# Forming the feed-forward weights' sums in DRAM with adding transfers instead of on GpSimd

## The chip, the cores and the metric

The kernel runs on one core of one Trainium2 chip. The metric is the device time of one execution in microseconds (us), as the median of several runs. The engines are named as in the profile: PE is TensorE's matrix multiply and PEld its weight load, DVE is VectorE, ACT is ScalarE, POOL is GpSimd, SP is SyncE, which here only issues transfers. "Raw" means a piece of weights as it lies in DRAM, 128 partitions by 1024 fp32 numbers, 512 KB.

## What is computed

Two transformer blocks over 512 tokens of width 1024, all in fp32, one sequence. In order: dilated-window attention ("dil"), differential attention ("diff"), an mLSTM and RG-LRU mixer ("ev"), cross-attention to 256 memory rows ("x0"), a feed-forward ("ff0"), sliding-window attention with sinks ("sw"), a second cross-attention ("x1") and a second feed-forward ("ff1"). Each has a norm before it and one after it. What the change touches is the feed-forward, and the norm of the input:

```python
def squared_relu_mlp(u, w1, w2):
    return jnp.square(jax.nn.relu(u @ w1)) @ w2      # w1: 1024 x 4096, w2: 4096 x 1024

def rmsnorm(x, g):
    x32 = x.astype(jnp.float32)
    y = x32 * lax.rsqrt(jnp.mean(x32 * x32, axis=-1, keepdims=True) + EPS)
    return y.astype(x.dtype) * g
```

## The kernel before

**Products.** An fp32 product is made of three matmuls (`mm3`): each operand is split into a high and a low part, and high x high, high x low and low x high are summed. The weights of the whole program lie in DRAM as one stream of tiles, `ws`, in the order in which they are used (`stream_order`). A tile is two halves of 512 KB. `weights` hands out the next tile, and through it `_take`, `_fill` and `_load` (L286 to L301) run ahead: SP loads a half into one of three buffers `raw`, ACT makes its high part (`whi`, L443) and DVE its low part (`wlo`, L444), each in four buffers. All loads are issued by SP in program order, two halves ahead of the one being split (three in a feed-forward).

**The feed-forward's second product** (`ff`) is done by Strassen and Winograd's scheme with seven products in place of eight: the weights of w2 are cut into 16 blocks, eight for each of ff0 and ff1, each of four quarters B11, B12, B21, B22 of 512 KB. The scheme needs four sums of quarters, T1 to T4. In the main loop, one turn for each block, PE does two tiles of the first product (`unit`), ACT squares the result, POOL forms the sums of activations s1, S2, S3, S4 (L1491), and PE does the three products with B11, T1 and B21 of the block before. The other four (with T4, T2, T3 and B22, named S4, S2, S3 and A22 after their left operand) come after the loop, over all blocks, and use the banks one after the other.

**The sums of weights** are made by `block` and `block_end` with POOL: SP loads the four quarters into SBUF (`quad`), POOL subtracts them in pieces of 128x256 (`less`, L354), and T3, T2 and T4 are stored to DRAM (`T<-quad`) and loaded again later (`raw<-T`). B11, T1 and B21 are split straight from `quad`. The dilated stage uses `less` too, for other weights, and is not touched there.

**The end of the main loops.** When the last product with T3 (S3) of a token tile is done, `done` adds its bank to the tile `acc` with a DVE addition (L1522); the product with B22 then continues in the same bank, so PE waits for that addition. Boundaries (`boundary`) do the norm after the stage and prepare the next.

**The first norms.** `first_u` loads four tiles of 128 tokens; `norm_T` multiplies by the gain, a part of the columns on POOL (the `cut`) and the rest on DVE, takes the squares on ACT, forms the reciprocal root on POOL (L468, L469, tile `rs`) and scales on DVE (L483). PE then transposes.

**What sets the order.** Each engine works through its own list in the order in which a scheduler placed the instructions; a transfer issued by SP is hardware-queued, one by POOL software-queued. Each of these two kinds has eight completion lanes (DMAHW0 to 7, DMASW0 to 7), and a transfer waits for the one that used its lane eight transfers earlier.

Of the kernel before, what the change touches and what calls it, by code (L numbers as in the profile page):

```python
# [12 lines left out]
F32 = mybir.dt.float32  # L13
# [3 lines left out]
ALU = mybir.AluOpType  # L17
AX = mybir.AxisListType

P = 128  # L20
S = 512
D = 1024
# [191 lines left out]
class Prog:  # L214
    def __init__(self, ctx, tc, a, out, stages):
        self.tc, self.nc, self.a, self.out, self.stages = tc, tc.nc, a, out, stages
        nc = self.nc
# [5 lines left out]
        blocks, self.groups, rest = [], {}, []  # L223
        for n, (key, kind, sel) in enumerate(self.order):
            if kind != "quad":
                self.halves += rest + [(n, 0), (n, 1)]
                rest = []
            elif sel[2] == P:
                g = self.groups.setdefault(key, [])
                if sel[0] == 0:  # L230
                    g.append([n])
                elif sel[1] == 0:
                    g[-1].append(n)
                elif sel[0] == 768:
                    first = [(b, name) for name in ("B11", "B21") for b in g[-1]]
                    rest[-2:-2] = first[:2]
                    rest += first[2:]
                    rest += [(b, name) for name in ("T1", "T2", "B22", "T3", "T4") for b in g[-1]]
            elif sel[1] == 0:
                blocks.append(n)  # L240
                self.halves += [(b, name) for b in blocks[-2:-1] for name in ("B11", "T1", "B21")]
                if len(blocks) == 8:
                    late = [(b, name + "'") for name in ("B22", "T2", "T3", "T4") for b in blocks]
                    self.halves += late[:5] + [(n, name) for name in ("B11", "T1", "B21")] + late[5:]
                    blocks = []
# [11 lines left out]

        self.ident = self.cp.tile([P, P], F32, name="ident")
# [28 lines left out]
    def _load(self):  # L287

        while self.loaded < len(self.halves) and self.loaded < self.done + self.depth:
            n, name = h = self.halves[self.loaded]  # L290
            self.loaded += 1
            if isinstance(name, str) and name[-1] != "'":
                continue
            r = self.wt[h] = self.wp.tile([P, 1024], F32, tag="raw", name="raw", bufs=3)
            if name == "B22'":
                src = self.a["ws"][n + 1, :, 1024:]
            elif isinstance(name, str):
                src = self.wt[n][name]
            else:
                src = self.a["ws"][n, :, name * 1024:(name + 1) * 1024]  # L300
            self.nc.sync.dma_start(out=r, in_=src)  # L301
# [19 lines left out]
    def weights(self, key=None):  # L321
# [5 lines left out]
        n = self.pos  # L327
        assert key in (None, self.order[n][0]), (self.order[n][0], key)
        self.pos += 1
        got = self._take(2)  # L330
        c = 256 if self.order[n][1] == "cols" else 512
        return n, *(Halved([g[x].rearrange("p (k c) -> p k c", c=c) for g in got]) for x in range(2))

    def block(self, n, pool):

        q = self.wt[n] = {}

        def new(name):
            q[name] = pool.tile([P, 1024], F32, tag="quad", name="quad", bufs=5)

        for m, name in enumerate(("B11", "B12", "B21", "B22")):
            new(name)
            self.nc.sync.dma_start(out=q[name], in_=self.a["ws"][n + m // 2, :, (m % 2) * 1024:(m % 2 + 1) * 1024])
        new("T3")
        q["T1"], q["T2"], q["T4"] = q["B12"], q["B22"], q["B21"]
        self.less(q["T3"], q["B22"], q["B12"])
        self.less(q["T1"], q["B12"], q["B11"])
        self.less(q["T2"], q["B22"], q["T1"])
# [6 lines left out]

    def block_end(self, n):

        q = self.wt[n]
        self.less(q["T4"], q["B21"], q["T2"])
        for name in ("T3", "T2", "T4"):  # L360
            d = q[name + "'"] = self.dr.tile([P, 1024], F32, tag=name, name=name, bufs=8)
            self.nc.sync.dma_start(out=d, in_=q[name])
# [454 lines left out]
    def dil(self):  # L817
        nc = self.nc
        y = []
        self.v_phase("dil")  # L820
        with self.vg, self.pool("rt_dil") as rp, self.pool("dl") as p:
# [114 lines left out]
            self.cuts = 3, 6  # L936
            for hp in range(8):
# [520 lines left out]
    def ff(self, l, stage):  # L1458
# [9 lines left out]
        self.block(blocks[0], p)  # L1468
# [3 lines left out]
        banks = {}  # L1472

# [4 lines left out]
        def operands(w, n, x2):  # L1478
# [9 lines left out]
            for out, x, z, op in ((s1, ya[:, h[1]], left["A22"][:, n], ALU.add), (left["S2"][:, n], s1, ya[:, h[0]], ALU.subtract),  # L1488
                                  (left["S3"][:, n], ya[:, h[0]], ya[:, h[1]], ALU.subtract),
                                  (left["S4"][:, n], yb, left["S2"][:, n], ALU.subtract)):  # L1490
                nc.gpsimd.tensor_tensor(out=out, in0=x, in1=z, op=op)  # L1491
# [6 lines left out]
        def products(q, ops):  # L1498
# [9 lines left out]
            self.block_end(blocks[q])  # L1508
            if q < 7:
                self.block(blocks[q + 1], p)  # L1510
# [11 lines left out]
        add = lambda out, ps: nc.vector.tensor_tensor(out=out, in0=out, in1=ps, op=ALU.add)  # L1522

        def done(name, t):
            ps = banks[name if name == "S4" else "A11"][t]
            if name in ("S4", "S2"):
                add(part(t, 1), ps)
            if name == "S2":
                self.boundary(t, (part(t, 0), part(t, 1)), self.h[:, t, :], stage, bo[0])
            elif name == "S3":  # L1530
                add(part(2 + t, 1), ps)
# [17 lines left out]
        for k, (name, i) in enumerate(steps):  # L1549
            if k == 5:  # L1550
                products(7, ops)
                first.close()
                acc.update({t: p.tile([P, D], F32, tag="quad", name="acc", bufs=5) for t in (2, 3, 0, 1)})
# [156 lines left out]
    def first_u(self):  # L1710
# [4 lines left out]
        with self.pool("x0") as p:  # L1715
# [8 lines left out]
            steps = [self.norm_T(xt[t], self.gpre, self.u, t, p, 4, 384 if t else 0) for t in range(2)]  # L1724
# [76 lines left out]
```

## Time and profile before

| what | value |
|---|---|
| median of 3 runs | 2335.98 us (2335.03 to 2336.01) |
| profiled execution, its own time | 2335.89 us |
| its span, first to last instruction | 2334.1 us |
| PE busy | 2287.8 us, 98% |
| DVE, ACT, POOL busy | 1432.2, 1140.8, 744.9 us |
| moved by SP's queue | 305.19 MB, 39.0% of the transfer engines' time |
| granted TensorE clock, mean | 0.999 |

The share of busy time is of the span; between the execution's own time and its span lie 1.8 us. The granted clock is that of the profile's rows, 1.0 for 2.4 GHz and 0.5 for 1.2 GHz. The stages begin about here in the span: diff at 636 us, ev at 900, x0 at 1140, ff0 at 1310, sw at 1650, x1 at 1830, ff1 at 2020.

### The profile page before, as it was taken

To read this page: it belongs to the slowest core of one execution; us is meant where nothing else is said; L and a number is where in the kernel's file an instruction comes from. 1 tells how busy PE (TensorE), PEld (TensorE's weight loads), DVE (VectorE), ACT (ScalarE), POOL (GpSimd) and SP (SyncE) were. 2 spreads that over 40 slices of the span, in tenths; PEclk is the share of its full clock that TensorE was granted. 3 is DMA by queue.
4 is the path that set the end of the run, shared out by engine and by line. 5 is a ranking of instruction groups with operands and counts; after the bars stand their busy time and mean duration, and the time that the engine had idled before them with its cause. 6 is when DMAs were issued, how large, how long until landed. Compare 5 with 4: busy or idle time off the path is not lost.

```text
span 2334.1 us, 33247 instructions
## 1 busy us (share of the span) xinstructions
PE 2287.8 (98%) x12168; PEld 1871.5 (80%) x12168; DVE 1432.2 (61%) x2522; ACT 1140.8 (49%) x2337; POOL 744.9 (32%) x799
## 2 busy tenths in 40 slices
PE   7999999999999999999999999999999999999998
PEld 6887777777878878777898888887966988888887
DVE  7665666666565555774745554468777744644476
ACT  4443544555444444553434454456456533544464
POOL 5962212121221113000200466661211200577640
PEclk9999999999999999999999999999999999999999
DMA  6335343332432222222342355555332332455554
GB/s 234 131 116 167 106 132 104 111 97 83 143 103 90 90 89 94 76 73 99 122 149 72 119 190 198 190 185 203 126 93 97 136 109 73 154 198 187 192 199 172
DMA packets 101284, 309.26 MB, mean 132 GB/s; under 512 B 14348, under 2 KB 20524, under 8 KB 101120
## 3 DMA queue, kind: packets, MB, share of 16 engines
q1 hardware_dynamic: 100320, 305.19, 39.0%
q0 software_dynamic: 800, 1.94, 0.3%
q8 instruction: 96, 1.57, 0.3%
q14 instruction: 68, 0.56, 0.1%
HBM read 253.59 MB, written 33.55 MB: 123 GB/s over the span
## 4 chain that ended last, share of the span: by engine, by line
PE 61%; DVE 5%; POOL 2%; ACT 2%; issue 2%; DMA 1%; SPq 0%; POOLq 0%; DVEq 0%; ACTq 0%
PE pj L370 13%; PE pj L371 13%; PE pj L372 13%; PE sc L371 3%; PE sc L370 3%; PE sc L372 3%; DVE wlo L444 1%; PE pv L370 1%; PE pv L371 1%; PE pv L372 1%; PE sc L1657 1%; PE sc L1022 1%; DVE h L521 1%; PE pt L491 1%; POOL rs L469 1%
## 5 line engine op out<-in xcount | busy, mean ns | idle before, releaser
L444 DVE TENSOR_TENSOR wlo<-raw,whi 128x1024 fp32r<-128x1024 f32 x348 | 452.4, 1308 | 301.0 <-ACT whi L443 284.9
L370 PE MATMUL pj<-uh,whi 128*128 128x512 f32 (+1 forms) x1424 | 561.7, 394 | 0.2 <-ACT ho L1348 0.2
L372 PE MATMUL pj<-uh,wlo 128*128 128x512 f32 (+1 forms) x1424 | 552.2, 388 | 2.1 <-DVE wlo L444 2.1
L371 PE MATMUL pj<-ul,whi 128*128 128x512 f32 (+1 forms) x1424 | 551.6, 387 | 0.0
L443 ACT ACTIVATE whi<-raw 128x1024 fp32r<-128x1024 f32 x348 | 364.9, 1057 | 352.9 <-PE pj L371 150.3
L354 POOL TENSOR_TENSOR quad<-quad 128x256 f32<-128x256 f32 x352 | 345.7, 1019 | 84.8 <-DVE wlo L444 37.8
L370 PEld LDWEIGHTS pj<-uh,whi 128*128 128x128 f32 x1424 | 267.6, 188 | 72.2 <-issue 17.3
L372 PEld LDWEIGHTS pj<-uh,wlo 128*128 128x128 f32 x1424 | 267.6, 188 | 61.1 <-issue 3.8
L371 PEld LDWEIGHTS pj<-ul,whi 128*128 128x128 f32 x1424 | 267.8, 188 | 52.9 <-issue 3.4
L603 POOL TENSOR_TENSOR ro<-rt 128x512 f32<-128x512 f32 x74 | 127.4, 1737 | 512.4 <-DVE rt L601 415.2
L466 POOL TENSOR_SCALAR rs<-ss 128x1 f32<-128x1 f32 x32 | 23.9, 747 | 542.0 <-ACT bq L512 541.6
L444 DVE TENSOR_TENSOR wlo<-quad,whi 128x1024 fp32r<-128x1024 f32 x90 | 125.3, 1395 | 76.2 <-ACT whi L443 76.1
L370 PE MATMUL sc<-whi,yh 128*128 128x512 f32 x384 | 151.7, 395 | 2.7 <-DVE acc L1522 2.6
L371 PE MATMUL sc<-wlo,yh 128*128 128x512 f32 x384 | 151.4, 394 | 1.1 <-DVE wlo L444 1.0
L372 PE MATMUL sc<-whi,yl 128*128 128x512 f32 x384 | 150.6, 393 | 0.0
L370 PE MATMUL pj<-whi,yh 128*128 128x512 f32 x360 | 141.9, 394 | 0.0
L371 PE MATMUL pj<-wlo,yh 128*128 128x512 f32 x360 | 140.7, 391 | 0.7 <-DVE wlo L444 0.7
L372 PE MATMUL pj<-whi,yl 128*128 128x512 f32 x360 | 140.7, 391 | 0.0
L443 ACT ACTIVATE whi<-quad 128x1024 fp32r<-128x1024 f32 x90 | 95.0, 1058 | 85.8 <-PE pj L371 33.0
L370 PEld LDWEIGHTS sc<-whi,yh 128*128 128x128 f32 x384 | 72.3, 188 | 20.9 <-ACT whi L443 2.0
L371 PEld LDWEIGHTS sc<-wlo,yh 128*128 128x128 f32 x384 | 72.4, 189 | 17.1 <-DVE wlo L444 2.8
L372 PEld LDWEIGHTS sc<-whi,yl 128*128 128x128 f32 x384 | 72.5, 189 | 15.0 <-DVE yl L444 0.2
(420 smaller groups left out, 4434.3 us busy)
## 6 DMA issues: line engine op xcount, KB each, us to landing
raw<-in_ws_dram SPq DMA_DIRECT2D x300, 512.0 KB, 3.7
quad<-in_ws_dram SPq DMA_DIRECT2D x88, 512.0 KB, 6.2
T<-quad SPq DMA_DIRECT2D x48, 512.0 KB, 3.0
raw<-T SPq DMA_DIRECT2D x48, 512.0 KB, 3.8
qk<-ro SPq DMA_DIRECT2D x256, 64.0 KB, 2.0
vd<-vo SPq DMA_DIRECT2D x24, 256.0 KB, 3.9
gpre<-in_gains_dram SPq DMA_DIRECT2D x8, 512.0 KB, 5.2
v<-vd SPq DMA_DIRECT2D x8, 512.0 KB, 5.0
```

The lines of the kernel that those rows point to most:

```text
L354: self.nc.gpsimd.tensor_tensor(out=out[:, cs], in0=x[:, cs], in1=y[:, cs], op=ALU.subtract)
L370: self.nc.tensor.matmul(ps, lhsT=ah, rhs=bh, start=first and k == 0, stop=False, **kw)
L371: self.nc.tensor.matmul(ps, lhsT=ah, rhs=bl, start=False, stop=False, **kw)
L372: self.nc.tensor.matmul(ps, lhsT=al, rhs=bh, start=False, stop=last and k == n - 1, **kw)
L443: self.nc.scalar.activation(out=dst[0], in_=src, func=AF.Copy)
L444: self.nc.vector.tensor_sub(out=dst[1], in0=src, in1=dst[0].bitcast(F32))
L466: nc.gpsimd.tensor_scalar(out=r[:, 0:1], in0=ss[:, 0:1], scalar1=ss[:, 1:2], scalar2=EPS, op0=ALU.add, op1=ALU.add)
L469: nc.gpsimd.tensor_tensor(out=r[:, 1:2], in0=r[:, 0:1], in1=self.mhalf[:, 0:1], op=ALU.pow)
L491: nc.tensor.transpose(pt[:, k * P:(k + 1) * P], b[:, (4 * g + k) * P:(4 * g + k + 1) * P], self.ident)
L521: nc.vector.scalar_tensor_tensor(out=h, in0=b, scalar=r, in1=h, op0=ALU.mult, op1=ALU.add)
L603: nc.gpsimd.tensor_tensor(out=o, in0=t[0], in1=t[1], op=op)
L1022: nc.tensor.matmul(ps[:, :n], lhsT=q[hs, 0, i * P:n], rhs=q[hs, 1, :n], start=True, stop=True)
```

## The change

It removes `block` and `block_end`. A list of 128 steps (`sums`, 64 for each feed-forward) forms the same sums in DRAM: a step is either a plain copy of 512 KB, DRAM to DRAM, issued by SP, or a transfer that adds its source to a tile in DRAM (`accum_op=add`), issued by POOL. [...] `weights` issues one step for each tile it hands out, from the dilated heads on (`self.paced`), and what is left at the start of a feed-forward is issued there (`background`). By the list, the 64 steps of ff0 are issued by the end of ev's output weights; those of ff1 go with x0, ff0's first weights, sw and x1, and 3 are left at the start of ff1. Every piece, B11, T1 and B21 too, is now loaded as `raw`. At the end of S3, ACT copies the bank to a tile `u3` and POOL subtracts it in two pieces, in place of the DVE addition. The tiles `acc` have a tag of their own. In `first_u`, the first two norms use no POOL columns (the second had 384).

```diff
--- before.py
+++ after.py
@@ -220,7 +220,7 @@
         self.wt = {}
 
         self.halves, self.ready, self.loaded, self.done, self.depth = [], [], 0, 0, 2
-        blocks, self.groups, rest = [], {}, []
+        blocks, self.groups, rest, sums = [], {}, [], []
         for n, (key, kind, sel) in enumerate(self.order):
             if kind != "quad":
                 self.halves += rest + [(n, 0), (n, 1)]
@@ -238,10 +238,11 @@
                     rest += [(b, name) for name in ("T1", "T2", "B22", "T3", "T4") for b in g[-1]]
             elif sel[1] == 0:
                 blocks.append(n)
-                self.halves += [(b, name) for b in blocks[-2:-1] for name in ("B11", "T1", "B21")]
+                self.halves += [(b, name + "'") for b in blocks[-2:-1] for name in ("B11", "T1", "B21")]
                 if len(blocks) == 8:
                     late = [(b, name + "'") for name in ("B22", "T2", "T3", "T4") for b in blocks]
-                    self.halves += late[:5] + [(n, name) for name in ("B11", "T1", "B21")] + late[5:]
+                    self.halves += late[:5] + [(n, name + "'") for name in ("B11", "T1", "B21")] + late[5:]
+                    sums += self.sums(blocks)
                     blocks = []
 
         def pool(name, **kw):
@@ -255,6 +256,7 @@
         self.sm = pool("sm")
         self.dr = pool("dr", space=bass.MemoryType.DRAM)
 
+        self.todo, self.paced, self.summed = iter(sums), False, 0
         self.ident = self.cp.tile([P, P], F32, name="ident")
         make_identity(nc, self.ident)
         self.mhalf = self.cp.tile([P, 8], F32, name="mhalf")
@@ -292,8 +294,8 @@
             if isinstance(name, str) and name[-1] != "'":
                 continue
             r = self.wt[h] = self.wp.tile([P, 1024], F32, tag="raw", name="raw", bufs=3)
-            if name == "B22'":
-                src = self.a["ws"][n + 1, :, 1024:]
+            if isinstance(name, str) and name[0] == "B":
+                src = self.part_of(n, name)
             elif isinstance(name, str):
                 src = self.wt[n][name]
             else:
@@ -328,38 +330,46 @@
         assert key in (None, self.order[n][0]), (self.order[n][0], key)
         self.pos += 1
         got = self._take(2)
+        if self.paced:
+            self.background()
         c = 256 if self.order[n][1] == "cols" else 512
         return n, *(Halved([g[x].rearrange("p (k c) -> p k c", c=c) for g in got]) for x in range(2))
 
-    def block(self, n, pool):
-
-        q = self.wt[n] = {}
-
-        def new(name):
-            q[name] = pool.tile([P, 1024], F32, tag="quad", name="quad", bufs=5)
-
-        for m, name in enumerate(("B11", "B12", "B21", "B22")):
-            new(name)
-            self.nc.sync.dma_start(out=q[name], in_=self.a["ws"][n + m // 2, :, (m % 2) * 1024:(m % 2 + 1) * 1024])
-        new("T3")
-        q["T1"], q["T2"], q["T4"] = q["B12"], q["B22"], q["B21"]
-        self.less(q["T3"], q["B22"], q["B12"])
-        self.less(q["T1"], q["B12"], q["B11"])
-        self.less(q["T2"], q["B22"], q["T1"])
+    def part_of(self, n, name):
+
+        m, c = int(name[1]) - 1, int(name[2]) - 1
+        return self.a["ws"][n + m, :, c * 1024:(c + 1) * 1024]
+
+    def sums(self, blocks):
+
+
+        steps = ((("T1", "B11"), ("T3", "B22")), (("T1", "B12"), ("T3", "B12")), (("T2", "T1"),), (("T2", "B22"),),
+                 (("T4", "T2"),), (("T4", "B21"),))
+        return [(blocks[at - k], name, src, k % 2) for at in range(len(blocks) + 5) for k in (0, 2, 4, 1, 3, 5)
+                if 0 <= at - k < len(blocks) for name, src in steps[k]]
+
+    def background(self, n=1):
+
+        for _ in range(n):
+            step = next(self.todo, None)
+            if step is None:
+                return
+            b, name, src, adds = step
+            self.summed += 1
+            q = self.wt.setdefault(b, {})
+            src = self.part_of(b, src) if src[0] == "B" else q[src + "'"]
+            if adds:
+                ins = self.nc.gpsimd.dma_start(out=q[name + "'"], in_=src, accum_op=ALU.add)
+            else:
+                d = q[name + "'"] = self.dr.tile([P, 1024], F32, tag=name, name=name, bufs=16)
+                ins = self.nc.sync.dma_start(out=d, in_=src)
+            self.tc.keep_in_program_order(ins)
 
     def less(self, out, x, y):
         out, x, y = (z.rearrange("p a b -> p (a b)") if len(z.shape) == 3 else z for z in (out, x, y))
         for c in range(4):
             cs = slice(c * 256, (c + 1) * 256)
             self.nc.gpsimd.tensor_tensor(out=out[:, cs], in0=x[:, cs], in1=y[:, cs], op=ALU.subtract)
-
-    def block_end(self, n):
-
-        q = self.wt[n]
-        self.less(q["T4"], q["B21"], q["T2"])
-        for name in ("T3", "T2", "T4"):
-            d = q[name + "'"] = self.dr.tile([P, 1024], F32, tag=name, name=name, bufs=8)
-            self.nc.sync.dma_start(out=d, in_=q[name])
 
     def mm3(self, ps, pairs, first=True, last=True, between=None, **kw):
 
@@ -934,6 +944,7 @@
 
             osb = {}
             self.cuts = 3, 6
+            self.paced = True
             for hp in range(8):
                 if hp:
                     plan(hp - 1)
@@ -1465,11 +1476,11 @@
         p = outer.enter_context(self.pool(f"ff{l}"))
         self.depth = 3
         left = {n: p.tile([P, 16, 256], F32, name=n) for n in ("S3", "A22")}
-        self.block(blocks[0], p)
         p2 = inner.enter_context(self.pool(f"fs{l}"))
         left.update({n: p2.tile([P, 16, 256], F32, name=n) for n in ("S4", "S2")})
         p1 = first.enter_context(self.pool(f"fr{l}"))
         banks = {}
+        self.background(8 * 8 * (l + 1) - self.summed)
 
         def square(out, ps, tmp):
             nc.scalar.activation(out=tmp, in_=ps, func=AF.Relu)
@@ -1485,9 +1496,9 @@
             square(yb, ps[:, h[0]], yb)
             square(left["A22"][:, n], ps[:, h[1]], left["A22"][:, n])
             s1 = p1.tile([P, 256], F32, tag="s1", name="s1", bufs=3)
-            for out, x, z, op in ((s1, ya[:, h[1]], left["A22"][:, n], ALU.add), (left["S2"][:, n], s1, ya[:, h[0]], ALU.subtract),
+            for out, x, z, op in ((s1, ya[:, h[1]], left["A22"][:, n], ALU.subtract), (left["S2"][:, n], s1, ya[:, h[0]], ALU.subtract),
                                   (left["S3"][:, n], ya[:, h[0]], ya[:, h[1]], ALU.subtract),
-                                  (left["S4"][:, n], yb, left["S2"][:, n], ALU.subtract)):
+                                  (left["S4"][:, n], yb, left["S2"][:, n], ALU.add)):
                 nc.gpsimd.tensor_tensor(out=out, in0=x, in1=z, op=op)
             x1 = self.pair()
             res = {"A11": [z[:, h[0]] for z in x1], "A12": [z[:, h[1]] for z in x1], "S1": [z[:, h[n % 2]] for z in x2]}
@@ -1505,9 +1516,6 @@
                     tok = slice(t * P, (t + 1) * P)
                     self.mm3(banks[name][t], [([z[:, tok] for z in ops[j][name]], (hi[:, j, :], lo[:, j, :])) for j in range(2)],
                              first=q == 0, skip_group_check=True)
-            self.block_end(blocks[q])
-            if q < 7:
-                self.block(blocks[q + 1], p)
 
         ops = []
         for q in range(8):
@@ -1519,16 +1527,20 @@
         banks["S4"] = [self.ps("pj") for _ in range(2)]
         acc, bo, late = {}, [], []
         part = lambda t, c: acc[t][:, c * 512:(c + 1) * 512]
-        add = lambda out, ps: nc.vector.tensor_tensor(out=out, in0=out, in1=ps, op=ALU.add)
+        add = lambda out, ps, op=ALU.add: nc.vector.tensor_tensor(out=out, in0=out, in1=ps, op=op)
 
         def done(name, t):
             ps = banks[name if name == "S4" else "A11"][t]
             if name in ("S4", "S2"):
-                add(part(t, 1), ps)
+                add(part(t, 1), ps, ALU.add if name == "S4" else ALU.subtract)
             if name == "S2":
                 self.boundary(t, (part(t, 0), part(t, 1)), self.h[:, t, :], stage, bo[0])
             elif name == "S3":
-                add(part(2 + t, 1), ps)
+                o = bo[0].tile([P, 512], F32, tag="u3", name="u3", bufs=2)
+                self.copy(o, ps, "s")
+                for c in range(2):
+                    cs = slice(c * 256, (c + 1) * 256)
+                    nc.gpsimd.tensor_tensor(out=part(2 + t, 1)[:, cs], in0=part(2 + t, 1)[:, cs], in1=o[:, cs], op=ALU.subtract)
             elif name == "A22":
                 self.boundary(2 + t, (ps, part(2 + t, 1)), self.h[:, 2 + t, :], stage, bo[0])
 
@@ -1550,7 +1562,7 @@
             if k == 5:
                 products(7, ops)
                 first.close()
-                acc.update({t: p.tile([P, D], F32, tag="quad", name="acc", bufs=5) for t in (2, 3, 0, 1)})
+                acc.update({t: p.tile([P, D], F32, tag="acc", name="acc", bufs=4) for t in (2, 3, 0, 1)})
                 for t in range(2):
                     self.copy(part(2 + t, 1), banks["S1"][t], "s")
                 for t in range(2):
@@ -1721,7 +1733,7 @@
                     self.gpre = self.gain(p, GAINS[self.stages[0]][0], "gpre")
                 elif t == 1:
                     self._load()
-            steps = [self.norm_T(xt[t], self.gpre, self.u, t, p, 4, 384 if t else 0) for t in range(2)]
+            steps = [self.norm_T(xt[t], self.gpre, self.u, t, p, 4, 0) for t in range(2)]
             steps[0]()
             steps[1]("pj")
             steps = [self.norm_T(xt[t], self.gpre, self.u, t, p, 4, 384) for t in range(2, NT)]
```

At the start, POOL lists these before the change (`rs` are the reciprocal roots, `bu<-xt,gpre` the multiplication by the gain):

```order
L468 TENSOR_SCALAR rs<-ss_106 128x1 [waits Activation_49]
L480 TENSOR_TENSOR bu<-xt,gpre 128x384 [waits DMAHW2_49,DMAHW1_49]
L469 TENSOR_TENSOR rs<-rs,mhalf 128x1 [waits Pool_49]
L468 TENSOR_SCALAR rs<-ss_115 128x1 [waits Activation_49]
L469 TENSOR_TENSOR rs<-rs,mhalf 128x1 [waits Pool_49]
L480 TENSOR_TENSOR bu<-xt,gpre 128x384 [waits DMAHW5_49]
```

And these with it:

```order
L478 TENSOR_SCALAR rs<-ss_106 128x1 [waits Activation_49]
L479 TENSOR_TENSOR rs<-rs,mhalf 128x1 [waits Pool_49]
L478 TENSOR_SCALAR rs<-ss_115 128x1 [waits Activation_49]
L479 TENSOR_TENSOR rs<-rs,mhalf 128x1 [waits Pool_49]
L490 TENSOR_TENSOR bu<-xt,gpre 128x384 [waits DMAHW5_49,DMAHW1_49]
```

The multiplication between the two steps of the first root is gone from POOL; DVE does all 1024 columns of the second tile.

Where the differential stage begins, POOL listed these before the change (`mask_d`, `tmp<-in_lam_dram` and `subln` are small transfers which that stage needs):

```order
L468 TENSOR_SCALAR rs<-ss_5860 128x1 [waits Activation_49]
L469 TENSOR_TENSOR rs<-rs,mhalf 128x1 [waits Pool_49]
L627 DMA mask_d<-in_mask_d_dram 128x512 [waits DMASW1_49,DMASW0_49,DVE_49]
L992 DMA tmp<-in_lam_dram 128x256
L627 DMA subln<-in_subln_dram 128x1
```

And these with it:

```order
L478 TENSOR_SCALAR rs<-ss_5906 128x1 [waits Activation_49]
L479 TENSOR_TENSOR rs<-rs,mhalf 128x1 [waits Pool_49]
L362 DMA T_4242<-in_ws_dram 128x1024 [waits DMASW5_49]
L362 DMA T_4377<-in_ws_dram 128x1024 [waits DMASW6_49]
L637 DMA mask_d<-in_mask_d_dram 128x512 [waits DMASW7_49,DVE_49]
L1003 DMA tmp<-in_lam_dram 128x256 [waits DMASW0_49]
L637 DMA subln<-in_subln_dram 128x1 [waits DMASW1_49]
L613 TENSOR_TENSOR ro<-rt 128x512 [waits DVE_49] x2
L362 DMA T_4560<-in_ws_dram 128x1024 [waits DMASW2_49]
```

Two adding transfers stand ahead of the small ones, and each of the small ones waits for a lane.

In x0, where the memory's weights are used, SP's list with the change is this (before it holds the rows `raw` alone):

```order
L365 DMA T_10405<-in_ws_dram 128x1024 [waits DMAHW2_49]
L303 DMA raw<-in_ws_dram 128x1024 [waits DMAHW7_49,DVE_49]
L303 DMA raw<-in_ws_dram 128x1024 [waits DMAHW0_49,DVE_49]
L365 DMA T_10632<-in_ws_dram 128x1024 [waits DMAHW5_49]
L303 DMA raw<-in_ws_dram 128x1024 [waits DMAHW1_49,DMAHW6_49,DVE_49,Activation_49]
L303 DMA raw<-in_ws_dram 128x1024 [waits DMAHW3_49,DVE_49]
L365 DMA T_10711<-in_ws_dram 128x1024
L303 DMA raw<-in_ws_dram 128x1024 [waits DMAHW4_49,DVE_49,Activation_49]
L303 DMA raw<-in_ws_dram 128x1024 [waits DMAHW6_49,DMAHW2_49,DVE_49]
L365 DMA T_10790<-in_ws_dram 128x1024
```

A copy now stands ahead of every two loads, and the loads wait for the lanes that copies use too.

## Rows read from the trace of the kernel before

**Rows 1.** The page: busy us of each engine, and SP's queue (packets, MB, share).

```profile
PE 2287.8 (98%) x12168; PEld 1871.5 (80%) x12168; DVE 1432.2 (61%) x2522; ACT 1140.8 (49%) x2337; POOL 744.9 (32%) x799
...
q1 hardware_dynamic: 100320, 305.19, 39.0%
```

**Rows 2.** POOL's row L354 alone, in ff0 and ff1: busy us (instructions).

```profile
1300.00:1600.00 300.00, 118.14 (x128) 1.00 0.54 189
2000.00:2300.00 300.00, 119.20 (x128) 1.00 0.57 196
```

**Rows 3.** Stretches of 50 us; busy us (count): PE, PEld, DVE, ACT, POOL; clock; DMA.

```profile
1450.00:1500.00 50.00, 50.00 (x222) 41.40 (x221) 24.35 (x22) 23.88 (x43) 36.47 (x43) 1.00 0.55 189
1550.00:1600.00 50.00, 49.34 (x216) 39.95 (x215) 42.70 (x45) 33.52 (x46) 16.95 (x15) 1.00 0.61 215
1600.00:1650.00 50.00, 47.40 (x219) 38.33 (x218) 39.28 (x44) 30.00 (x46) 12.74 (x13) 1.00 0.46 164
2250.00:2300.00 50.00, 49.24 (x214) 39.49 (x213) 41.52 (x51) 34.87 (x51) 4.47 (x7) 1.00 0.70 241
```

**Rows 4.** PE's waits over the whole run: total us, times, longest.

```profile
PE pt L491 <- DVE bu L483: 17.7, 7, 11.8
```

**Rows 5.** Timeline of the start: start us, us, instruction [idle before it, what ended it].

```profile
5.82 1.23 DVE L480 TENSOR_TENSOR bu<-xt,gpre 128x1024 f32<-128x1024 f32 x1 [5.82 <-DMA gpre<-in_gains_dram]
8.70 0.83 DVE L480 TENSOR_TENSOR bu<-xt,gpre 128x640 f32<-128x640 f32 x1 [1.65 <-DMA xt<-in_x_dram]
...
8.81 1.56 POOL L480 TENSOR_TENSOR bu<-xt,gpre 128x384 f32<-128x384 f32 x1 [2.83 <-DMA xt<-in_x_dram]
...
10.94 0.75 DVE L483 TENSOR_SCALAR bu<-bu,rs 128x1024 f32<-128x1024 f32 x1 [1.42 <-POOL rs L469]
...
11.75 1.54 PE L491 MATMUL pt<-ident,bu 128*128 128x128 f32 x6 [11.75 <-DVE bu L483]
```

**Rows 6.** Timeline, last block of ff0: POOL's sum, then PE.

```profile
1538.12 4.00 POOL L354 TENSOR_TENSOR quad<-quad 128x256 f32<-128x256 f32 x4 [2.96 <-DVE wlo L444]
...
1573.65 0.50 PE L371 MATMUL pj<-wlo,yh 128*128 128x512 f32 x1 [0.37 <-DVE wlo L444]
```

**Rows 7.** Timeline, end of S3 in ff0, and a POOL piece of 128x256.

```profile
1623.58 0.68 DVE L1522 TENSOR_TENSOR acc<-acc,sc 128x512 f32<-128x512 f32 x1
...
1624.41 0.47 PE L370 MATMUL sc<-whi,yh 128*128 128x512 f32 x1 [1.60 <-DVE acc L1522]
...
1542.08 0.74 POOL L1491 TENSOR_TENSOR s<-ya,A 128x256 f32<-128x256 f32 x1
```

**Rows 8.** The page, transfers: out<-in, issuing queue, count, KB, median us to landing.

```profile
raw<-in_ws_dram SPq DMA_DIRECT2D x300, 512.0 KB, 3.7
...
T<-quad SPq DMA_DIRECT2D x48, 512.0 KB, 3.0
...
qk<-ro SPq DMA_DIRECT2D x256, 64.0 KB, 2.0
```

**Rows 9.** Timeline, start of diff: POOL's issues, and DVE waiting for one.

```profile
635.12 0.95 POOL L627 DMA_DIRECT2D mask_d<-in_mask_d_dram  x1
636.08 0.55 POOL L992 DMA_DIRECT2D tmp<-in_lam_dram  x1
...
639.50 0.36 DVE L996 TENSOR_TENSOR tmp<-tmp 128x64 f32<-128x64 f32 x2 [0.82 <-DMA tmp<-in_lam_dram]
...
641.62 0.69 DVE L601 TENSOR_TENSOR rt<-sc,cos 128x512 f32<-128x512 f32 x1 [0.82 <-PE sc L372]
```

**Rows 10.** Memory weights of x0: a stretch, and ACT waiting for a load.

```profile
1160.00:1194.70 34.70, 34.70 (x292) 34.70 (x290) 20.20 (x22) 16.10 (x20) 0.00 (x0) 1.00 0.58 196
...
1164.95 1.06 ACT L443 ACTIVATE whi<-raw 128x1024 fp32r<-128x1024 f32 x1 [2.93 <-DMA raw<-in_ws_dram]
```

**Rows 11.** Timeline, start of sw: SP's issues of q and PE's first score.

```profile
1695.53 5.46 SPq L1640 DMA_DIRECT2D q<-ro  x8
...
1702.39 0.48 PE L1657 MATMUL sc<-kd,q 64*128 64x128 f32 x2
```

## Prediction

> **What bounds the kernel now.** I read the page first: PE is busy 2287.8 of 2334.1 us [rows 1], so some 46 us are all that can come from any wait, and the change leaves PE's matmuls as they are. POOL is the engine that the change relieves: the pieces of row L354 in the two feed-forwards take 118.14 and 119.20 us [rows 2], all removed. The next view, stretches of 50 us, tells whether they bound anything. In the main loop of ff0 PE is busy 50.00 of 50.00 us with 222 matmuls, while POOL has 36 us [rows 3]: POOL is not the bound there, and removing it gives nothing. Only the edges are not full. From 1550 PE does 216 matmuls in place of 222, which is 6 x 0.225 = 1.35 us; from 1600 it is idle 2.60 us; in ff1 from 2250 it does 214, so 1.8 us [rows 3]. So the feed-forwards can give 5.75 us at most. Last I read PE's waits: the longest is the start, 11.8 us for the first scaled tile [rows 4].
>
> The profiled execution took 2335.89 us, 0.09 under the median of the runs; its span is 1.8 us less. I make the sum against it.
>
> **First norms.** POOL's multiplication begins at 8.81 and ends at 10.37; the root's second step stands behind it, so DVE scales at 10.94 after idling 1.42, and PE starts at 11.75 [rows 5]. The change takes the multiplication out from between. The root is then done before DVE is free; DVE multiplies 1024 columns where it did 640, 1.23 us for 0.83 [rows 5], from 8.70 to 9.93, and scales right behind. That is 10.94 - 9.93 = 1.0 us earlier. **-1.0** (0 if the weights then come late, to -1.4, the whole idle time).
>
> **Sums in the main loops.** 256 POOL pieces, 237.3 us [rows 2], lie beside a full PE: 0. SP's transfers change from 128 loads and 48 stores to 112 loads in the loops' time; the 64 copies and 64 additions lie earlier. PE stays full: 0. The edge of the last block is another matter: there the sum of 4.00 us runs at 1538, and the low parts of later weights come late, costing PE 0.37 us at 1573.65 [rows 6] and some smaller gaps, 1.35 us in the stretch [rows 3]. Without quarters to load and store the loads come sooner. I take **-1.0** of the 1.35 for ff0; in ff1 part of the 1.8 us is a wait for a bank, which stays, and I take **-0.5**.
>
> **End of S3.** PE waits 1.60 us for DVE's addition, which begins at 1623.58 behind a low part [rows 7]. A copy by ACT frees the bank earlier, so this goes. But ACT's next row then reads `acc`, which is ready only after two POOL pieces of 0.74 us [rows 7], and the high part of the next weights stands behind it on ACT: 1.5 us come back. **0** (from -1.6 to +1.5).
>
> **The new transfers.** The trace has no copy from DRAM to DRAM and no adding transfer, so I bound both. SP's queue moved 305.19 MB in 39.0% of the engines' time [rows 1]: 0.39 x 2334.1 / 305.19 x 0.524 = 1.56 us of all engines for 512 KB in one pass. A copy costs 1.56 if read and write go in one pass, 3.1 if in two. An addition reads twice and writes once: 1.56 to 4.7. I take the middles, 2.3 and 3.1; a store and a load, the nearest rows, land in 3.0 and 3.7 us with their fixed part [rows 8], which fits neither end better. On POOL an issue costs up to 0.95 [rows 9]; 64 of them are 61 us where 237 were removed.
>
> Where do 128 of these meet something? In the attention heads and the output products there is one step for each tile of at least 48 matmuls of 0.225 us, 10.8 us; with two loads (3.1) and a step (4.7 at worst) it is under 8 us: 0. The exception is the memory's weights, eight tiles in each of x0 and x1. Their matmuls are half as long: 34.70 us for 292 [rows 10], 0.119 each, 48 for a tile, 5.7 us. Loads already land just in time there (ACT idles 2.93 for one at 1164.95) [rows 10]. With two loads at 1.56 and a step: by my middles x0 has 6 copies and 2 additions, 20 + 25 = 45 us of 45.6, and x1 3 and 5, 22.4 + 25 = 47.4. There are about 3 us of slack in the split pieces. So it just fits, and I take **+0.5** for x0 and **+0.7** for x1 as the odd late load.
>
> The Trainium skill ("DMA: Bandwidth & Descriptors", Latency and other measured facts) gives 207 to 214 GB/s for copies between tensors in DRAM whose row pitch is not one of the slow ones; by it, an estimate, a copy is 2.5 us, which no run here shows yet. By that the sum of x0 would be 1 us longer and no more.
>
> **Small transfers at two edges.** Two additions now stand ahead of `mask_d`, `lam` and `subln` on POOL. Behind two issues of 0.95 the lam arrives 2 us later than 639.50, and DVE, which waits for it, has until 641.62 when PE's next result comes [rows 9]: nearly free. But the 64 KB transfers after it land in 2.0 us alone [rows 8], and the diff stage's first score and the first score of sw (PE at 1702.39, the issue of the last q ending 1701) [rows 11] follow the landing without slack. A copy in their way delays them by part of its 2.3 us: **+0.5** each, +1.0 (0 to +4).
>
> **Sum:** -1.0 - 1.0 - 0.5 + 0 + 0.5 + 0.7 + 1.0 = -0.3, so 2335.89 - 0.3 = **2335.6 us**. A measurement of this kernel tells some 0.2% from no change, 4.7 us.
>
> **Rivals.**
>
> *B, slower: transfers fill the engines with the memory's weights.* Place: eight tiles of x0 and of x1. It decides from 5.7 - 2 x 1.56 = 2.6 us for a step on. At the high bounds, 3.1 and 4.7, x0 needs 25 + 6 x 3.1 + 2 x 4.7 = 53 us of 45.6, x1 25 + 3 x 3.1 + 5 x 4.7 = 57.8: +7.4 and +12.2, less 3 us of slack each, about +13.6. With the gains of the forecast that gives **2349 us**. For it: loads land just in time there, at 0.58 share of the transfer engines [rows 10]. Against: a store into DRAM is no slower than a load [rows 8], so one direction is cheap. The Trainium skill ("Collectives: The Full Stack", The bandwidth ceiling: the fold count and why AG ≠ RS ≠ AR) says that an adding transfer needs two source reads through one ring and runs at about half of a copy's rate; by it and the page's figure for copies an addition would be some 4.9 us, an estimate, which is this rival's end. No row of before has such a transfer. **17%.**
>
> *C, faster: all edges fill up and nothing comes late.* -1.0 at the start, -1.35 in ff0's last block, -1.6 at S3 (ACT has time for the pieces), -0.8 in ff1: -4.75, **2331.1 us**. For it: each of these waits has a row [rows 3, 5, 7]. Against: ACT's order behind S3. **13%.**
>
> *D, a little slower: small transfers queue behind big ones.* Every 64 KB transfer on a path without slack (first scores of diff and sw, lam) waits for a whole copy or addition, 1.6 to 3.1 us each, two or three times: +3 to +7 with nothing gained at S3, **2341 us**. For it: completion lanes are shared, so a small transfer waits for the one eight earlier. Against: most small transfers land long before their use. **12%.**
>
> *A, the forecast*, to which belongs that the change does not do what it says, because POOL's work was hidden all along [rows 3]: **58%.**
>
> **How the numbers follow.** The likeliest is A, 2335.6. The range reaches down to C (2331.0) and up through D, into the half of B's span where only x1 overflows (+12.2 - 3 = +9.2): 2345.0. Above it lies most of B, some 12%, and below it some 6%. Faster by over 0.2% means under 2331.3: half of C and a sliver of A, 0.10. Slower means over 2340.7: B, half of D and the rest from A's upper end, 0.24. Same: 0.66.
>
> **What would show it.** Right: DVE's first scaling at about 9.9 and PE's first row at 10.7; POOL without rows of L354 after the dilated weights; the stretch 1450 to 1500 with 222 matmuls as before; in the page's list of transfers a copy that lands in 3 to 5 us. B shows as waits of PE or ACT for `raw` in x0 and x1 and a transfer share near 1 there; D as a later first score in diff and sw; C as stretches 1550 to 1650 with 222 matmuls each. Wrong would be any loss in the main loops, which I count as full, or a term of over 3 us in the dilated heads.

## The result, and the profile after

The changed kernel takes **2372.57 us** (median of 4 runs, 2365.73 to 2373.6) against 2335.67 (4 runs of before): slower, 1.0146 times, interval 1.0134 to 1.0158. I had forecast 2335.6 and a range to 2345. The profiled execution took 2365.73, the shortest of the four; what follows accounts for its 30 us, not for the 37 of the median.

The page of the changed kernel: busy time, the queues, and the transfers with their time to landing.

```profile
PE 2301.4 (97%) x12168; PEld 1880.5 (80%) x12168; DVE 1411.2 (60%) x2518; ACT 1143.4 (48%) x2341; POOL 564.6 (24%) x614
...
q1 hardware_dynamic: 96736, 305.19, 38.4%
q0 software_dynamic: 10016, 35.49, 8.9%
...
T<-in_ws_dram POOLq DMA_DIRECT2D x64, 512.0 KB, 7.4
...
T<-in_ws_dram SPq DMA_DIRECT2D x32, 512.0 KB, 5.6
```

POOL lost 180 us of work, and SP's queue moves the same bytes [rows 1]. The adding transfers are the growth of queue q0. PE is busy 13.6 us longer with the same 12168 matmuls [rows 1], and the mean granted clock is 0.991 in place of 0.999; the other 16 us of the 30 are idle time. PE's waits over the whole run, those that are new against [rows 4]:

```profile
PE sc L1033 <- DMA qk<-ro: 6.1, 1, 6.1
PE pj L381 <- DVE wlo L454: 4.0, 5, 0.9
...
PE sc L1669 <- DMA q<-ro: 2.4, 1, 2.4
PE pj L380 <- ACT whi L453: 2.2, 3, 1.0
```

PE's order is the same in both kernels but for two matmuls that come eight places earlier, so each matmul's start can be subtracted from that of before. The difference changes in few places ("half clock" is a granted clock of 0.5, 1.2 GHz):

| place (time in before) | change of the delay, us | what is seen there |
|---|---|---|
| start to 577 | -2.8 | scaling earlier; no half-clock stretch at 574 |
| first score of diff, 654 | +10.3 | wait of 6.1, then half clock |
| ev, 940 and 975 | +3.1 | small tables (`rgw` and others) late behind an addition, +1.5; half clock, +1.6 |
| memory's norm ahead of x0, 1109 | +2.4 | wait of 2.6 in place of 1.8; half clock |
| memory's weights of x0, 1171 to 1175 | +4.7 | three waits, half clock |
| ff0 | -1.2 | -1.2 last block, -1.9 and +1.9 at S3 |
| first scores of sw, 1703 | +5.9 | wait of 2.4, then half clock |
| memory's weights of x1, 1855 to 1869 | +7.6 | waits, half clock |
| ff1 and between the places | -0.2 | |

Together +29.8, and the spans differ by 29.9. The main loops are as full as before, 222 matmuls in 50 us. Stretches of the changed kernel (columns as in [rows 3], then GB/s):

```profile
650.00:660.00 10.00, 3.91 (x13) 2.36 (x11) 2.35 (x3) 0.50 (x2) 1.80 (x2) 0.84 0.87 227
660.00:670.00 10.00, 10.00 (x31) 6.46 (x32) 4.35 (x17) 3.00 (x8) 0.00 (x0) 0.65 0.08 32
...
1860.00:1900.00 40.00, 35.21 (x262) 33.93 (x261) 20.45 (x23) 16.39 (x22) 9.86 (x11) 0.91 0.97 253
1450.00:1500.00 50.00, 50.00 (x222) 41.42 (x221) 21.50 (x23) 26.02 (x48) 12.20 (x16) 1.00 0.49 148
```

The kernel before, at the place of the first two rows:

```profile
650.00:660.00 10.00, 10.00 (x45) 7.19 (x45) 5.41 (x17) 3.63 (x10) 0.00 (x0) 1.00 0.66 203
```

The second row of the changed kernel is the one that I had no term for: the wait is over, PE is busy all 10 us, the transfers are quiet (0.08), and yet the granted clock is 0.65, so a part of the stretch ran at 1.2 GHz and only 31 matmuls were done. Of the 10.3 us at this place 6.1 are the wait and 4.2 come behind it. Over the run the 13.6 us of longer busy time are this part: matmul by matmul, 14.9 us are lost in half-clock stretches, and before lost 1.5 in its one at 574.

What made the first score late, on the timelines of POOL, DVE and PE:

```profile
632.34 1.84 POOL L362 DMA_DIRECT2D T<-in_ws_dram  x2
633.84 0.94 POOL L637 DMA_DIRECT2D mask_d<-in_mask_d_dram  x1
634.45 0.90 POOL L1003 DMA_DIRECT2D tmp<-in_lam_dram  x1
...
646.44 4.53 POOL L613 TENSOR_TENSOR ro<-rt 128x512 f32<-128x512 f32 x2 [10.55 <-DVE rt L611]
650.91 0.90 POOL L362 DMA_DIRECT2D T<-in_ws_dram  x1
```

```profile
642.63 0.36 DVE L1007 TENSOR_TENSOR tmp<-tmp 128x64 f32<-128x64 f32 x2 [6.72 <-DMA tmp<-in_lam_dram]
```

```profile
657.63 0.76 PE L1033 MATMUL sc<-qk 64*128 64x128 f32 x2 [6.09 <-DMA qk<-ro]
```

`lam`, issued at 634.45, lands 8.1 us later, just behind the second addition (641.68); before it took 3.4 [rows 9]. DVE idles 6.72 for it with the rotations queued behind. A third addition, issued at 650.91, then runs beside the eight 64 KB pieces of `qk`: the first four land 1.9 to 2.1 us after their issue, the last four 4.1 to 5.5.

At sw one addition stood beside the pieces of `q`, again on POOL's timeline:

```profile
1714.61 0.91 POOL L362 DMA_DIRECT2D T<-in_ws_dram  x1
```

The pieces issued up to then landed 2.0 us after their issue, the seven issued from 1715.26 to 1720.71 after 4.7 to 7.1 us.

And the additions of x1, on POOL's timeline:

```profile
1863.61 6.86 POOL L362 DMA_DIRECT2D T<-in_ws_dram  x8
```

All eight go out in 6.9 us, right behind the boundary's norm. By the list of steps they are the additions of x1's memory weights and of its queries, tiles that are used one after the other, long after the burst: SP's copies wait in line with the loads, but nothing ties an addition to its tile, and POOL issues all of them as soon as its list reaches them. From 1870.1 to 1897.5 they land one by one, some 3.9 us apart, and the raw loads beside them at 3.8 to 3.9, where tiles ask for two loads in 5.7 us.

### The profile page after: what moved, and what is told of

Same layout as the page of the kernel before. It is cut to its first block, busy times and chain, and to the rows that moved or that the text cites. A ratio compares the mean times of both kernels' runs of the same rounds, so it can differ in the third digit from the quotient of the medians.

```text
span 2364.0 us, 33064 instructions
## 1 busy us (share of the span) xinstructions
PE 2301.4 (97%) x12168; PEld 1880.5 (80%) x12168; DVE 1411.2 (60%) x2518; ACT 1143.4 (48%) x2341; POOL 564.6 (24%) x614
## 5 line engine op out<-in xcount | busy, mean ns | idle before, releaser
L454 DVE TENSOR_TENSOR wlo<-raw,whi 128x1024 fp32r<-128x1024 f32 x396 | 501.8, 1272 | 356.7 <-ACT whi L453 344.9
L453 ACT ACTIVATE whi<-raw 128x1024 fp32r<-128x1024 f32 x396 | 416.5, 1056 | 395.2 <-PE pj L381 189.0
L372 POOL TENSOR_TENSOR quad<-quad 128x256 f32<-128x256 f32 x96 | 108.3, 1168 | 0.0
L362 POOL DMA_DIRECT2D T<-in_ws_dram x64 | 55.2, 1027 | 149.2 <-DMA T<-T 109.2
L454 DVE TENSOR_TENSOR yl<-ya,yh 128x256 fp32r<-128x256 f32 x32 | 19.6, 613 | 118.5 <-ACT yh L453 118.5
```

The costliest lines, as they stand in the source:

```text
L362: ins = self.nc.gpsimd.dma_start(out=q[name + "'"], in_=src, accum_op=ALU.add)
L372: self.nc.gpsimd.tensor_tensor(out=out[:, cs], in0=x[:, cs], in1=y[:, cs], op=ALU.subtract)
L453: self.nc.scalar.activation(out=dst[0], in_=src, func=AF.Copy)
L454: self.nc.vector.tensor_sub(out=dst[1], in0=src, in1=dst[0].bitcast(F32))
```

## The experiments

**Edge theory**: time is lost only where a transfer without slack, or the memory's weights, stand beside additions, which POOL's list lets go together; half clock follows the waits. **Volume rival**: the additions cost wherever they run.

**1. The norms alone.** Before, with

```diff
-self.norm_T(xt[t], self.gpre, self.u, t, p, 4, 384 if t else 0)
+self.norm_T(xt[t], self.gpre, self.u, t, p, 4, 0)
```

> The kernel before with the first two norms wholly on DVE and nothing else of the change. Both theories: the change's own trace shows PE's first row 1.15 us earlier than before and 1.8 us by 20 us of the span, so 2334 to 2335, 1 to 2 us under before. If the gain is lost later (weights late), 2335.7.

2335.26 against 2336.97 us, ratio 1.0 (0.9991 to 1.001): too small for the timing. The profile has the first matmul at 10.59 (before 11.75 [rows 5]) and is 1.0 to 2.5 us ahead of before up to 970; from there on it is between 0.6 ahead and 0.1 behind in this execution.

**2. No additions, 3. copies in their place, 4. no steps.**

```diff
 if adds:
-    ins = self.nc.gpsimd.dma_start(out=q[name + "'"], in_=src, accum_op=ALU.add)
+    continue                                                                  # run 2
+    ins = self.nc.gpsimd.dma_start(out=q[name + "'"], in_=src)                # run 3
```

Run 4 skips every step and loads B12, B22, B12 and B21 for T1 to T4.

> The changed kernel without the 64 adding transfers; the 64 copies stay where they are, so T1, T2 and T4 hold their first term only and T3 lacks one (that part of the feed-forwards is left out). Edge theory: the time is lost in a few places without slack (first scores of diff and sw, small tables of diff and ev, the memory's weights of x0 and x1), where additions that GpSimd releases together take the transfer engines, and each wait of PE is followed by a stretch at half clock. Copies alone are spaced by SP's own loads: 2330 to 2340, diff's first score without a wait of 6 us, no wait for weights in x0 and x1. Volume rival: the loss of 30 to 37 us goes with the bytes moved by steps, of which copies are about 2.3 of 5.4 us each pair: 2348 to 2356.

> The changed kernel with each adding transfer made a plain copy of the same source to the same place, issued by GpSimd at the same point of its list (the sums are left out). Edge theory, with release in bursts as the cause: bursts stay, each transfer takes about 2.3 in place of 3.2 us of the engines, so part of the loss stays: 2345 to 2362. If the adding itself is what is dear, 2335 to 2342. If the issue from GpSimd is (waits in its list), 2365 to 2373 as in the changed kernel.

> The changed kernel without any of the 128 steps: the second product's pieces T1 to T4 are loaded from the weights themselves (the sums are left out). It shows what the sums cost and what GpSimd's relief gives. Edge theory: about 2331 to 2333 (before, less 1.8 at the start, less 2 or so at the ends of the main loops, less the half-clock stretch at 574). If other parts of the change (signs, the copy and two GpSimd pieces at S3, quarters loaded through raw) cost something by themselves, over 2336.

Without additions 2336.04 us, ratio 0.9997 (0.9987 to 1.0006); as copies 2345.0, 1.0038 (1.0023 to 1.0053); without steps 2334.41, 0.999 (0.9981 to 1.0). So the 64 copies cost 1.6 us in the medians, which the intervals do not separate from nothing, and nearly all of the loss is the additions. As plain copies at the same points, in the same bursts, they cost about 9 us, as additions 37. The queue's row of run 3 gives a reason:

```profile
q0 software_dynamic: 10016, 35.49, 5.1%
```

The same packets took 5.1% of the engines' time in place of 8.9%. Before, 0.3% were other transfers, so one addition is 0.086 x 2364.0 / 64 = **3.18 us** of all engines and the copy from POOL 0.048 x 2343.0 / 64 = **1.76 us**. Copies from SP come to (0.401 x 2333.7 - 0.357 x 2331.5) / 64 = 1.62, by the shares of SP's queue in runs 2 and 4. These are the times of packets, and they do not simply add up: in the burst of x1 an addition and a load landed every 3.9 us together. Run 3 was on the lower edge of what bursts alone should have cost: burst and price both count.

**5. Off the edges.** `weights` asks a table for the number of steps; the table is in the expectation.

```diff
-    self.background()
+    self.background(self.pace(self.order[n][0]))
```

> The changed kernel with all 128 steps, but issued elsewhere: three with each tile of the dilated heads, none with the dilated output weights, the first four and last two tiles of diff, the first three of ev, the memory's weights of x0 and x1 and the first three of sw, two with each tile of ff0's first product. Edge theory: an addition costs only where a transfer without slack or the memory's weights stand beside it, so nearly all of the loss goes: 2333 to 2340, no wait of PE for q or qk, mean granted clock 0.998. Volume rival (slow additions cost wherever they run, since the bytes and the engines' time are the same): 2360 to 2373.

2345.49 us, 1.0043 (1.0028 to 1.0058): 27 of the 36 us gone, with all additions still there, but 9 left, more than expected. The trace shows why: a place in the program is not a time on POOL. Three additions that belong to the queries and output weights of x0 went out early and together, behind the norm, into the memory's weights:

```profile
1161.18 2.65 POOL L369 DMA_DIRECT2D T<-in_ws_dram  x3 [0.20 <-issue]
```

Three waits of 0.9 us followed, and PE was 3.6 us later behind them. It was the same at 1849, +1.8, and an addition at 1704 met sw's q, +2.1 at that score. Two at 209 met the first dilated scores, +3.2. Half clock did not follow here: the granted clock stayed at 1.00 behind the three waits and behind the one of 2.0 us at sw.

```profile
1175.00:1195.00 20.00, 17.36 (x139) 16.60 (x138) 12.02 (x12) 9.63 (x13) 0.00 (x0) 1.00 0.64 198
1705.00:1720.00 15.00, 12.98 (x56) 8.43 (x55) 6.87 (x31) 5.08 (x21) 3.42 (x4) 1.00 0.83 176
```

**6. Off the memory's weights only, 7. on them only.**

> The changed kernel with no steps at the memory's weights of x0 and x1; two in place of one with each tile of ff0's first product, the rest as in the changed kernel. Edge theory: the delays of 4.8 us in x0 and some 6 us in x1 go and those of diff, ev and sw stay: 10 to 12 us under the changed kernel of the same time, 2355 to 2362. Volume rival: no gain, 2365 to 2373.

> The complement: the steps are placed as in the run off the edges, but with one for each of the eight tiles of memory weights in x0 and in x1, and one in place of two with each tile of ff0's first product. Edge theory: only the delay of the memory's weights stays, so 10 to 13 us over the run off the edges, 2344 to 2352, with PE waiting for weights there and a share of the transfer engines over 0.9 in x1. Volume rival: as the changed kernel, 2360 to 2373.

Run 6: 2366.24 us, 1.0128 (1.0112 to 1.0143), a miss. x0's delay was gone, x1's stayed at 6.7: five additions of tiles around it, by the list those of sw's last output weights and of x1's queries and output weights, went out at the same place:

```profile
1865.72 4.32 POOL L366 DMA_DIRECT2D T<-in_ws_dram  x5
```

The rest went at the start (3.5 us), at 857 (3.1) and in ev (1.6), all places with half-clock stretches that the changed kernel's profile does not have or has shorter. Run 7: 2356.61, 1.0087 (1.007 to 1.0104): 11.1 over run 5, as expected of 10 to 13 (2344 to 2352 in all was not met, since run 5 itself came 5 us higher). In x0 the transfer engines' share was 0.94, the clock 0.87. Before and run 7:

```profile
1160.00:1200.00 40.00, 40.00 (x316) 39.08 (x314) 23.12 (x24) 17.65 (x22) 0.00 (x0) 1.00 0.57 192
```

```profile
1160.00:1200.00 40.00, 32.84 (x228) 31.05 (x227) 18.31 (x22) 14.10 (x17) 6.16 (x8) 0.87 0.94 242
```

**8. Off the edges, second placement, 9. the edge of diff put back.**

> All 128 steps, moved once more, since the run off the edges still had additions that GpSimd released late: three with each tile of the dilated heads but for the first four and last two, two with diff's tiles 4 to 13 and ev's 3 to 9, two with each tile of ff0's first product, one with the first tiles of x0's and x1's output weights, none with the memory's weights, the queries of x0 and x1, sw, or the first tiles of a stage. Edge theory: no burst at 1161, 1704 and 1849 any more, so 5 to 9 us under the run off the edges: 2334 to 2340, no wait for weights in x0 and x1. Volume rival (an addition costs something everywhere): 2344 to 2349, as the run off the edges.

> As the run before it, but steps with the four tiles of the dilated output weights and with the first tiles of diff as in the changed kernel (one each), so that one addition stands ahead of the small tables of diff in GpSimd's list and one between the rotations ahead of the first scores. Edge theory: that edge alone brings back 6 to 11 us, a wait of PE at the first score of diff and a stretch at half clock behind it: 2341 to 2350. Volume rival: no difference to the run before it.

Run 8: **2334.98 us**, 0.9998 (0.9988 to 1.0007), no different from before, with all 128 steps and 9.1% of the engines' time in q0 (8.9% in the changed kernel). The volume rival falls; the 0.0008 between this ratio and run 4's lies within the intervals. Run 9: 2345.28, 1.0036 (1.0022 to 1.005). Ten us come back, not all at the edge meant. Against run 8, 5.2 us are at diff's first score, a wait of 2.4 with half clock behind it; 3.8 are at the dilated scores, with waits of 2.8 at two of them beside a burst of three additions that run 8 does not have; and 2.6 are around the memory's norm, where no step stands near in either run. The rows for 650 to 670, run 8 and then run 9:

```profile
650.00:670.00 20.00, 19.97 (x92) 14.23 (x91) 13.46 (x37) 7.99 (x20) 3.85 (x3) 1.00 0.44 134
```

```profile
650.00:670.00 20.00, 17.64 (x71) 12.38 (x70) 7.93 (x22) 6.46 (x14) 1.87 (x2) 0.83 0.49 131
```

Not every half-clock stretch is the additions' doing. Run 1, which changes no transfer, has one in ev with PE busy and the transfers quiet, and run 2, without additions, has one at the memory's norm (run 1, then run 2):

```profile
970.00:980.00 10.00, 10.00 (x31) 6.42 (x30) 3.78 (x9) 5.66 (x15) 0.00 (x0) 0.83 0.02 6
```

```profile
1105.00:1115.00 10.00, 7.84 (x34) 6.39 (x33) 7.28 (x8) 5.17 (x8) 4.83 (x6) 0.83 0.20 67
```

At these places the two runs lose 1.6 and 2.0 us. So the 1.6 us at 975 and the 2.4 at the memory's norm in the table above are not shown to be a price of the additions. The delays at the other places are gone in run 2 and in run 8.

**10. The end of S3 on DVE**, on top of run 8.

```diff
-for c in range(2):
-    cs = slice(c * 256, (c + 1) * 256)
-    nc.gpsimd.tensor_tensor(out=part(2 + t, 1)[:, cs], in0=part(2 + t, 1)[:, cs], in1=o[:, cs], op=ALU.subtract)
+nc.vector.tensor_tensor(out=part(2 + t, 1), in0=part(2 + t, 1), in1=o, op=ALU.subtract)
```

> The run before it but one (all steps off the edges, placed the second time) with the subtraction at the end of S3 done by DVE from the copy, in one piece, in place of the two GpSimd pieces. In the changed kernel ACT idled 3.6 us there for GpSimd, and PE waited 0.56 and 0.76 us for weights behind it in ff0. If the two GpSimd pieces give back what the early copy saves, those waits go and the stretch of ff0's end gains 1 to 1.5 us: 2333 to 2334.5, a little under the kernel before (0.05 to 0.15%), at the limit of what is measurable. If the waits come from DVE's own order or from late loads, they stay and the time is 2334.5 to 2336.

**2333.61 us**, 0.9988 (0.9979 to 0.9997): the one version under the kernel before, by 0.12%. In the changed kernel the two pieces stood like this, first POOL and then ACT waiting for them:

```profile
1637.91 3.53 POOL L1543 TENSOR_TENSOR acc<-acc,u 128x256 f32<-128x256 f32 x2 [7.31 <-ACT u L281]
```

```profile
1641.47 0.63 ACT L522 ACTIVATE bq<-acc 128x512 bf16<-128x512 f32 x1 [3.64 <-POOL acc L1543]
```

A piece takes 1.77 us here, not the 0.74 of [rows 7], and PE then waits 0.56 for a high part and 0.76 for a low part:

```profile
1643.20 0.50 PE L380 MATMUL sc<-whi,yh 128*128 128x512 f32 x1 [0.56 <-ACT whi L453]
1644.46 0.50 PE L381 MATMUL sc<-wlo,yh 128*128 128x512 f32 x1 [0.76 <-DVE wlo L454]
```

In run 10 the first of these is gone and the second is 0.27.

## Why the prediction was wrong

- **Main loops, 0**: right. 222 matmuls per 50 us; POOL's 237 us were hidden, and run 4, without any sums, is at 0.999.
- **First norms, -1.0**: right, -1.15 at PE's first row [rows 5].
- **Last block, -1.0 and -0.5**: right in ff0 (-1.2), near in ff1 (-0.8, given back at its S3).
- **End of S3, 0**: right, -1.9 and +1.9 in ff0. The saving was read too small by 0.3 and the piece's duration by over half, so that they cancel is in part luck.
- **The prices, 2.3 and 3.1**: the addition right at 3.18, by luck, since 3.1 was the middle of two bounds without a row for either; the copies 1.6 to 1.8, near the low end. The estimate of 2.5 from the Trainium skill's "DMA: Bandwidth & Descriptors" (Latency and other measured facts) lies above them. The ratio, 1.8, agrees with the rule that I set beside rival B, from the Trainium skill's "Collectives: The Full Stack" (The bandwidth ceiling: the fold count and why AG ≠ RS ≠ AR), told there of a collective's ring: an add reads two sources and runs at about half of a copy's rate. Its level, an estimate of 4.9 us, does not: 3.18 was measured.
- **"Small transfers at two edges", +1.0**: this step failed most. I priced the issues ahead of `lam` (0.95 each) and not the transfers: behind two additions it took 4.7 us longer to land than before, not the 2 of the issues, and SP's first piece of `qk` came 3.3 us late. I took a part of a copy for `qk`, and the addition that POOL issued behind its two rotations cost the last pieces 2.1 to 3.5 us. The two first scores came to +16.2 in place of +1.0. The small tables of ev, which stand behind an addition too, had no term and cost 1.5.
- **"One step for each tile", +0.5 and +0.7**: failed by the reading of POOL's list. I took a step to run when its tile is handed out. On POOL an addition waits for its source and its lane, not for the tile; between two norms POOL has little else and runs ahead. With the measured prices, 1.62 and 3.18, my sums would still say that it fits or nearly does, 41 us of 45.6 in x0 and 46 of 45.6 in x1; but they spread the additions over the tiles. The eight came back to back, and beside them one load landed every 3.8 us where a tile asks for two in 5.7. Measured: +4.7 and +7.6.
- **What I left out**: the long waits (6.1 at diff, 2.6 at the memory's norm, 2.4 at sw) and the repeated short ones at the memory's weights were each followed by a stretch at half clock in this execution; with the stretch in ev, and less the one of before, that makes the 13.6 us of busy time. The trace of before has such a stretch at 574 to 577, and I put it in no term. It does not come behind every wait, as run 5 shows.
- **The rivals**: B's place and D's mechanism both came true. B's size agrees (12.3 us in x0 and x1 against 13.6), but by luck: it asked for 3.1 and 4.7 us for a copy and an addition, and what filled the engines was the burst. Its 2349 should have been 2348 by the forecast's other terms. I gave each a chance as if the others were then out, though they share a cause, and priced D without the clock, so the top of the range held neither's sum.

## What to carry to other kernels

A transfer that only fills idle time was free here where every transfer beside it had slack, and dear where one had none; look for those with zero slack first, and put nothing beside them. A step written beside one engine's work but issued from another engine's list is not paced by that work: read what its row waits for there, and what else the list holds until the next real wait. Price a wait of a full TensorE with what its clock does afterwards, from a place where the trace already shows it, and as a chance, since not every wait was followed by half clock.

## What the runs showed that I had not expected

An adding transfer of 512 KB takes 3.18 us of all transfer engines and a median of 7.4 us to land, a plain copy from the same list 1.76 and 5.0. Its issue holds POOL for a median of 0.87 us, that of the plain copy for 0.54. A small transfer behind additions in POOL's queue landed only after them (8.1 us for `lam`); whether the queue's order or the shared engines held it back was not tried. Small transfers of SP's queue beside one addition landed in 4.1 to 5.5 us in place of 2.0 at diff, and in up to 7.1 at sw. What makes the executions of the changed kernel differ by 8 us (2365.73 to 2373.6) was not tried; the half-clock stretches, which fell at other places in run 6 than in the changed kernel, are a candidate: the mean granted clock was 0.991 in the shortest execution and 0.989 in the other three.
